# Two transformer blocks on one core: first attention scores inside the value projection, preparation spread over the head loop, low halves of some weights and sums of squares by other engines

## Chip, cores and metric

The kernel runs on one core of a Trainium2 chip. The metric is the device time of one execution in microseconds (us). Before the change it is 2415.28 us, the median of three runs (2414.47 to 2416.01). The profiled execution has a span of 2413.3 us from its first to its last instruction and a time of its own of 2415.17 us; the 1.9 us between them lie around the program. Five engines work side by side, each through its own instructions in order: TensorE (PE: matrix products and transposes), VectorE (DVE), ScalarE (ACT), GpSimd (POOL) and SyncE (SP, which issues loads). DMA engines move data; a DMA issued from POOL's queue can add into its destination.

## What is computed

Two residual networks, one behind the other, over 512 positions of width 1024, in float32. The first ("block 1", two layers) has differential attention and a gated linear recurrence, an MLP of width 4096 and a gate with a per-layer embedding; it ends with an RMS norm. The second ("block 2", two layers) is cut here to the part that the change touches:

```
hn   = rms_norm(h, g_pre_mix)
u, q, k, v, iq, ik, iw = split(hn @ w_in_2[l])          # the last three: the "index"
logits = einsum('qhd,sd->qhs', iq, ik) * IDX_DIM**-0.5
score  = einsum('qh,qhs->qs', iw, relu(logits))          # -inf for later chunks
top_idx = top_k(score, 128)                              # which keys a query may see
s = einsum('qhd,qkhd->qhk', q, k[top_idx]) * HEAD_DIM**-0.5
o = einsum('qhk,qkhd->qhd', softmax(s), v[top_idx])      # 8 heads of 64
y = pool_mixer(u)                                        # windowed means, a small product
h = h + norm(concat(y, o) @ w_out_2[l])
h = h + norm(square(relu(norm(h) @ w_ff1_2[l])) @ w_ff2_2[l])
```

The kernel does not gather: it computes all scores of a query and adds a bias that is a large negative number for each key outside the 128 highest index scores.

## The kernel before

**Split operands.** Each float32 factor is kept as a high half, which TensorE takes exactly, and a low half that holds the rest. A product of 128 by 128 weights with 512 columns is three matmuls: high by high, high by low, low by high. I call these three one *step*.

**Weights.** `PLAN` lists all pieces of weights in the order of use. `w_load` loads a piece into `raw` by SP's queue. `w_conv` makes `wh` (ACT, line 206) and `wl` in one of three ways: VectorE subtracts `raw - wh`; or ACT writes `-wh` (line 212) and a DMA from POOL's queue adds the piece from memory (line 215); or POOL subtracts in two halves (line 219). The second way is that of `w_in`, `w_out`, `w_in_2`, `w_out_2` and whatever is in `BY_DMA`; the third is that of the index pieces of layer 1.

**Order.** The order of TensorE's instructions is the order in which the Python code emits them (`Lane` chains them). `run(generator, n, at=...)` emits steps of a product and calls a hook behind the n-th; `weave(acts, g, n)` spreads a list of small acts over `n` steps of a generator. The other engines are ordered by the framework's scheduler by priority: what is emitted first goes first, unless `urgent` (or `tc.high_priority`) lifts it.

**Attention of block 2** is `mix2`. Behind the index scores VectorE chooses the 128 keys in 16 rounds for three groups of queries: `V.max` finds eight values, `V.match_replace` marks them; then three `tensor_scalar` turn the marks into the bias (tiles `ac`). Meanwhile TensorE runs the projections of k, q (`four(1024, ...)`) and v (`four(1536, ev_v)`). `prep_d`, `prep_q(j)` and `prep_k(j, c)` transpose two heads' queries and keys into `qs` and `ks` (ACT writes the high half, VectorE the low one). Before the change these stand as hooks in the v projection:

```
run(four(1536, ev_v), at={7: lambda: bcast(s_[:, 0:4], sb), 8: lambda: prep_d(0, 0),
                          9: lambda: prep_d(0, 1), 13: lambda: prep_q(0),
                          19: lambda: prep_k(0, 0), 25: lambda: prep_k(0, 1)})
```

Then a loop over 32 pairs of head and query tile follows: `sco` (scores on TensorE), `sof` (softmax: VectorE adds the bias and takes the maximum, ACT takes the exponential and normalizes, tile `xe`), `ptr` (TensorE transposes the weights; ACT and VectorE write the halves of `pt`), `pv` (the product with v). `weave` puts 66 steps of `fill()` between them, which are the projection of `u`, the pool mixer and half of `w_out_2`.

**Norms.** `Stat.add` squares a tile on ACT (tile `q`) and adds it to `acc` (VectorE, or POOL at line 423 with `eng=G`); `Stat.mean` sums `acc` over the partitions with a product against `ones`. `st4` and `st5` are the sums behind block 1's last gate and behind each block-2 layer. At the end of layer 0 of block 2, `index(0)` and `index(1)` run the next layer's index product for each half of the positions while the norm behind the MLP (`post_norm` on VectorE, with `split` into the tiles `X`) is still being finished; I call that stretch the index stage.

## Time and profile before

| | us |
|---|---|
| median of three runs | 2415.28 |
| the profiled execution | 2415.17 |
| its span | 2413.3 |
| TensorE busy | 2368.2 |
| VectorE busy | 1298.3 |
| ScalarE busy | 1189.6 |
| GpSimd busy | 266.9 |

TensorE is busy for 98% of the span, so its waits add up to some 45 us. A row of waits names the engine's line, the instruction that released it, the sum of the waits, how many there are and the longest. A row of a timeline gives the start, the time from the start of the first to the end of the last of the instructions that are shown together, engine, line, operation, output and inputs (without numbers), the shape and how many; in brackets the idle time before it and who ended it. Starts of matmuls that follow each other give the pace of the engine; their own durations overlap.

### The profile page before, as it was taken

The page shows a single profiled execution, that of the slowest core. Times are in us where ns is not written, and L with a number is a line of the kernel's source. Part 1 is how long each engine was busy: PE and PEld are TensorE (multiplying, and loading weights), DVE is VectorE, ACT ScalarE, POOL GpSimd, SP SyncE. Part 2 cuts the span into 40 slices and gives each one's busy share as a digit, 9 for nine tenths or more (in the row PEclk, how much of TensorE's full clock was granted, in tenths as well). Part 3 has the DMA queues.
Part 4 walks back from the last instruction along what each step waited for, and adds up shares of the span by engine and source line. Part 5 has one row for each costly group of instructions (what it writes and reads, how often), then busy time and mean ns, then how long its engine had stood idle before and what let it go on. Part 6 is the DMA issues. An engine that isn't in the chain of part 4 may idle for free.

```text
span 2413.3 us, 30955 instructions
## 1 busy us (share of the span) xinstructions
PE 2368.2 (98%) x11740; PEld 1987.3 (82%) x11740; DVE 1298.3 (54%) x2543; ACT 1189.6 (49%) x2028; POOL 266.9 (11%) x478
## 2 busy tenths in 40 slices
PE   9999999999999999999999999999999999999999
PEld 6878888888887888888888788888898878888888
DVE  8586433435458643344469857323337975532434
ACT  7785322424688532233366786323326588432422
POOL 3310000000131000000033120000014411000000
PEclk9999999999999999999999999999999999999999
DMA  7743333232874433233257554333325737333231
GB/s 201 177 100 107 103 97 96 92 100 88 192 175 98 113 96 96 91 101 96 83 136 161 118 132 121 97 96 96 96 79 141 164 82 171 92 97 97 95 104 54
DMA packets 79141, 273.31 MB, mean 113 GB/s; under 512 B 8848, under 2 KB 11280, under 8 KB 78992
## 3 DMA queue, kind: packets, MB, share of 16 engines
q1 hardware_dynamic: 62288, 211.22, 27.8%
q0 software_dynamic: 16704, 60.11, 14.3%
q8 instruction: 92, 1.51, 0.3%
q14 instruction: 57, 0.47, 0.1%
HBM read 269.20 MB, written 2.10 MB: 112 GB/s over the span
## 4 chain that ended last, share of the span: by engine, by line
PE 78%; DVE 11%; ACT 6%; issue 2%; POOL 1%; DMA 1%; SPq 0%; DVEq 0%; ACTq 0%; POOLq 0%
PE B L131 78%; DVE ac L131 2%; DVE m L131 2%; ACT xe L672 1%; DVE fo L131 1%; DVE xe L131 1%; DVE X L131 1%; ACT wh L206 1%; DVE rn L131 1%; ACT xe L1280 1%; ACT wl L212 1%; DVE h L131 1%; DVE pt L131 1%; ACT pt L1300 0%; DVE acc L131 0%
## 5 line engine op out<-in xcount | busy, mean ns | idle before, releaser
L131 PE MATMUL B<-X,wh 128*128 128x512 f32 (+1 forms) x3200 | 970.6, 386 | 0.1
L206 ACT ACTIVATE wh<-raw 128x1024 fp32r<-128x1024 f32 (+2 forms) x374 | 391.0, 1047 | 802.6 <-PE B L131 786.7
L131 DVE TENSOR_TENSOR wl<-raw,wh 128x1024 fp32r<-128x1024 f32 (+2 forms) x260 | 315.8, 1215 | 720.6 <-ACT wh L206 715.8
L131 PEld LDWEIGHTS B<-X,wh 128*128 128x128 f32 x3200 | 578.6, 189 | 104.0 <-issue 4.1
L131 PE MATMUL B<-X,wl 128*128 128x512 f32 (+1 forms) x1600 | 611.5, 382 | 2.8 <-POOL wl L219 1.8
L131 PE MATMUL B<-F,wh 128*128 128x512 f32 (+1 forms) x2048 | 597.8, 376 | 0.0
L131 PEld LDWEIGHTS B<-F,wh 128*128 128x128 f32 x2048 | 376.5, 188 | 70.0
L131 PE MATMUL B<-F,wl 128*128 128x512 f32 (+1 forms) x1024 | 384.8, 376 | 0.0
L131 PEld LDWEIGHTS B<-X,wl 128*128 128x128 f32 x1600 | 301.1, 188 | 62.5 <-POOL wl L219 2.6
L131 PE MATMUL B<-wh,X 128*128 128x512 f32 (+2 forms) x960 | 291.2, 380 | 0.0
L131 PEld LDWEIGHTS B<-F,wl 128*128 128x128 f32 x1024 | 192.8, 188 | 34.8
L131 PEld LDWEIGHTS B<-wh,X 128*128 128x128 f32 x960 | 176.4, 191 | 30.8 <-issue 1.9
L131 PE MATMUL B<-wl,X 128*128 128x512 f32 (+2 forms) x504 | 180.5, 371 | 3.1 <-DVE X L131 1.6
L215 POOL DMA_DIRECT2D wl<-in_w x105 | 92.0, 876 | 449.3 <-ACT wl L212 316.8
L212 ACT ACTIVATE wl<-raw 128x1024 fp32r<-128x1024 f32 (+2 forms) x108 | 112.6, 1043 | 41.3 <-PE B L131 41.2
L131 DVE TENSOR_TENSOR f<-r 128x512 f32<-128x512 f32 (+1 forms) x136 | 88.2, 656 | 59.6 <-ACT r L591 59.6
L591 ACT ACTIVATE r<-B 128x512 f32<-128x512 f32 (+1 forms) x136 | 76.3, 566 | 80.9 <-PE B L131 78.4
L131 PEld LDWEIGHTS B<-wl,X 128*128 128x128 f32 x504 | 93.5, 191 | 19.8 <-DVE X L131 2.2
L131 PE MATMUL B<-ks,qs 128*128 128x256 f32 (+2 forms) x352 | 84.3, 334 | 4.7 <-DVE qs L131 2.0
L131 DVE TENSOR_TENSOR F<-f,F 128x512 fp32r<-128x512 f32 (+1 forms) x136 | 88.3, 654 | 0.9 <-ACT F L397 0.2
L408 POOL TENSOR_TENSOR v<-v,nhalf 128x4 f32<-128x4 f32 x3 | 3.1, 1035 | 760.3 <-DVE v L131 760.3
L397 ACT ACTIVATE F<-f 128x512 fp32r<-128x512 f32 (+1 forms) x136 | 81.3, 604 | 4.2 <-DVE f L131 1.8
(224 smaller groups left out, 2412.4 us busy)
## 6 DMA issues: line engine op xcount, KB each, us to landing
raw<-in_w SPq DMA_DIRECT2D x379, 512.0 KB, 3.5
wl<-in_w POOLq DMA_DIRECT2D x105, 512.0 KB, 7.8
F<-in_w POOLq DMA_DIRECT2D x8, 512.0 KB, 10.7
raw<-in_wx SPq DMA_DIRECT2D x8, 328.0 KB, 2.9
h<-in_xT SPq DMA_DIRECT2D x8, 256.0 KB, 6.1
raw<-in_wx SPq DMA_DIRECT2D x8, 256.0 KB, 2.7
pt<-in_gates SPq DMA_DIRECT2D x2, 512.0 KB, 5.3
p<-in_pT SPq DMA_DIRECT2D x4, 256.0 KB, 2.9
```

The costliest lines, as they stand in the source:

```text
L131: r = f(*a, **k)
L206: g = A.activation(h_[:, :n], r[:, :n], AF.Copy)
L212: g = A.activation(l_[:, :n], r[:, :n], AF.Copy, scale=-1.0)
L215: G.dma_start(l_[:, :n], where[i], accum_op=OP.add)
L397: A.activation(dst[:, 0, :], src, AF.Copy)
L408: st["rsqrt"] = G.tensor_tensor(y, v, nhalf[:, :y.shape[-1]], op=OP.pow)
L591: A.activation(r_[:, :n], p_, AF.Relu)
L672: A.activation(e[:, :n], e[:, :n], AF.Exp, scale=-1.0, bias=mn, accum_out=sums)
L1280: A.activation(e[:, :n], e[:, :n], AF.Copy, scale=sm[:, 1:2])
```

## The change

It has six parts.

1. Low halves of all index pieces of layer 1 are made by ACT's negative copy and an adding DMA of POOL's queue in place of POOL's subtraction.
2. The pieces of `w_out_2` with `k >= 4` (four in each layer, 2 of them for each half of the columns) get their low half from VectorE in place of ACT and the adding DMA.
3. In block 1's last layer the sums `st4` and `st5` of the last four tiles are emitted behind the gate's product instead of within its evictions, and `st5` adds on VectorE in place of POOL; the pool of tiles has room for more of them.
4. In layer 0 of block 2 the sums `st4` are taken out of `nxt4` (where POOL added) and put into the last eight steps of `index(1)`, on VectorE.
5. The v projection is emitted behind the definitions, with new hooks: `prep_q(0)` at step 11 and `prep_k(0, 0)` at 15 (13 and 19 before), the scores and softmaxes of pairs 0 and 1 at 21, 22, 28 and 29. The loop starts at pair 0 with no empty acts ahead.
6. In the loop the preparation of the next two heads is spread from four neighbouring places over five of eight places, the last of them in the first place of those heads themselves.

```diff
-BY_DMA += [e for e in PLAN if e[0] == "index" and e[1] == 0][:3]
+BY_DMA += [e for e in PLAN if e[0] == "index" and e[1] == 0][:3] + [e for e in PLAN if e[0] == "index" and e[1] == 1]
...
         if (PLAN[i][0] in ON_POOL and PLAN[i][0] != "index" and i > 5
+                and not (PLAN[i][0] == "w_out_2" and PLAN[i][3] >= 4)
                 and PLAN[i][:4] != ("w_in_2", 0, 512, 0)) or PLAN[i] in BY_DMA:
...
-        elif PLAN[i][0] == "index" and PLAN[i][1] == 1 or i <= 5:
+        elif i <= 5:
             for a in range(0, n, n // 2):
                 b = slice(a, a + n // 2)
-                g = G.tensor_sub(l_[:, b], r[:, b], h_[:, b].bitcast(F32))
-                if "rsqrt" in st:
-                    behind(g, st["rsqrt"].ins)
+                G.tensor_sub(l_[:, b], r[:, b], h_[:, b].bitcast(F32))
...
-                L = Tags(lp, prj=(C512, F32, 8), t=(C512, F32, 3),
-                         q=(C512, F32, 2), sb=(C512, F32, 1))
+                L = Tags(lp, prj=(C512, F32, 8), t=(C512, F32, 6),
+                         q=(C512, F32, 4), sb=(C512, F32, 1))
...
+                    def sums(k):
+                        st4.add(h[k])
+                        if last:
+                            st5.add(h[k], scale=col("g_final", 0, k))
...
-                        st4.add(h[k])
-                        if last:
-                            st5.add(h[k], scale=col("g_final", 0, k), eng=G)
+                        if not last or g == 0:
+                            sums(k)
...
+                    if last and g == 1:
+                        for k in range(4, 8):
+                            sums(k)
...
-            run(four(1536, ev_v), at={7: lambda: bcast(s_[:, 0:4], sb), 8: lambda: prep_d(0, 0),
-                                      9: lambda: prep_d(0, 1), 13: lambda: prep_q(0),
-                                      19: lambda: prep_k(0, 0), 25: lambda: prep_k(0, 1)})
...
+            run(four(1536, ev_v), at={7: lambda: bcast(s_[:, 0:4], sb), 8: lambda: prep_d(0, 0),
+                                      9: lambda: prep_d(0, 1), 11: lambda: prep_q(0),
+                                      15: lambda: prep_k(0, 0), 21: lambda: sco(0), 22: lambda: urgent(sof)(0),
+                                      25: lambda: prep_k(0, 1), 28: lambda: sco(1), 29: lambda: urgent(sof)(1)})
             n = H2 * T
-            acts = [lambda: None] * 3
+            acts = []
...
-            for j in range(-2, n + 1):
+            for j in range(0, n + 1):
                 m, r = divmod(j, 8)
                 nx = 0 <= j < n - 8
-                if 0 <= j + 1 < n:
+                if 1 < j + 1 < n:
                     act(urgent(sof), j + 1)
...
-                if nx and r in (1, 2):
-                    act(prep_d, m + 1, r - 1)
-                if nx and r == 2:
+
+                if nx and r in (2, 6):
+                    act(prep_d, m + 1, r // 4)
+                if nx and r == 4:
                     act(urgent(prep_q), m + 1)
-                if nx and r == 3:
+                if nx and r == 5:
                     act(urgent(prep_k), m + 1, 0)
-                if nx and r == 4:
-                    act(urgent(prep_k), m + 1, 1)
+                if 8 <= j < n and r == 0:
+                    act(urgent(prep_k), m, 1)
...
                 split(X4[k][:, :, ts], h[k][:, ts], col("g_pre_mix_2", l + 1, k))
-                st4.add(h[k][:, ts], ts, eng=G)
...
-                run(index(1), at={7: f(1, 3, 4), 15: f(1, 5, 6), 23: f(1, 7)})
+                def sums(ts, *ks):
+                    for k in ks:
+                        st4.add(h[k][:, ts], ts)
...
+                run(index(1), at={7: f(1, 3, 4), 15: f(1, 5, 6), 23: f(1, 7),
+                                  **{24 + i: lambda i=i: sums(HALVES[i // 4], i % 4 * 2, i % 4 * 2 + 1)
+                                     for i in range(8)}})
```

How it moves instructions is shown at three places. The first is TensorE at the first scores of block 2's attention in layer 0 (`<-ks,qs`). `B` are its output banks, `wh`, `wl` the halves of a weight, `X` the activations. Before, the scores stand behind the last step of the v projection (`<-wh,X`), among steps of the projection of `u` (`<-X,wh`):

```order
L131 MATMUL B_10807<-wl_10809,X_9783 128x512
L131 MATMUL B_10807<-wh_10808,X_9783 128x512
L131 MATMUL B_10987<-X_9520,wh_10845 128x512 x2
L131 MATMUL B_10987<-X_9520,wl_10846 128x512
L131 MATMUL B_10999<-ks_10921,qs_10885 128x256 x2
L131 MATMUL B_10988<-X_9520,wh_10845 128x512 x2
```

After:

```order
L131 MATMUL B_10805<-wh_10749,X_9749 128x512
L131 MATMUL B_10805<-wl_10750,X_9749 128x512
L131 MATMUL B_10805<-wh_10749,X_9749 128x512
L131 MATMUL B_10930<-ks_10902,qs_10879 128x256 x2
L131 MATMUL B_10806<-wh_10749,X_9749 128x512
L131 MATMUL B_10806<-wl_10750,X_9749 128x512
L131 MATMUL B_10806<-wh_10749,X_9749 128x512
```

The scores have moved up past ten steps of the v projection, one step of `u` and one group of transposes. From the transposes of `sn` at the head of the last third of that projection to the first scores there were 25 steps and four groups of four transposes, that of `sn` counted; now there are 14 steps and three groups. Layer 1 has the same order.

The second place is VectorE at the end of the choice of keys in layer 0. The last row of the choice is `MATCH_REPLACE`, the three `TENSOR_SCALAR` make the bias, `qs` and `ks` are the low halves of the first two heads. Before:

```order
L131 MATCH_REPLACE ac_9807<-m_10644,ac_9807 128x512
L131 TENSOR_SCALAR ac_9805<-ac_9805 128x256
L131 TENSOR_SCALAR ac_9806<-ac_9806 128x384
L131 TENSOR_SCALAR ac_9807<-ac_9807 128x512
L131 TENSOR_TENSOR qs_10885<-B_10880,qs_10885 64x512
L131 TENSOR_TENSOR qs_10886<-B_10880,qs_10886 64x512
L131 TENSOR_TENSOR ks_10921<-B_10916,ks_10921 128x512
L131 TENSOR_TENSOR ks_10954<-B_10949,ks_10954 128x512
```

After:

```order
L131 MATCH_REPLACE ac_9807<-m_10644,ac_9807 128x512
L131 TENSOR_SCALAR ac_9805<-ac_9805 128x256
L131 TENSOR_SCALAR ac_9806<-ac_9806 128x384
L131 TENSOR_SCALAR ac_9807<-ac_9807 128x512
L131 TENSOR_TENSOR qs_10879<-B_10874,qs_10879 64x512
L131 TENSOR_TENSOR qs_10880<-B_10874,qs_10880 64x512
L131 TENSOR_TENSOR ks_10902<-B_10897,ks_10902 128x512
L131 ISA xe_10937,mn_10938<-B_10930,kbias 128x128
```

Up to the first `ks` VectorE's order is the same; behind it the first softmax (`ISA xe`) now comes ahead of the second `ks`.

The third place is POOL in the index stage. Before, it subtracts for the index pieces (line 219) and adds sums (line 423):

```order
L219 TENSOR_TENSOR wl_15168<-raw_14934,wl_15168 128x256 x2
L219 TENSOR_TENSOR F_14930<-raw_14915,F_14929 128x328 x2
L219 TENSOR_TENSOR F_15187<-raw_15172,F_15186 128x328 x2
L423 TENSOR_TENSOR acc_12460<-acc_12460,q_15115 128x256
L423 TENSOR_TENSOR acc_12460<-acc_12460,q_15122 128x256
L219 TENSOR_TENSOR wh_15221<-raw_15191,wh_15221 128x256 x2
L423 TENSOR_TENSOR acc_12460<-acc_12460,q_15154 128x256
```

After:

```order
L407 TENSOR_TENSOR rs_15037<-v_15035,nhalf 128x2
L216 DMA F_14926<-in_wx 128x656
L216 DMA wl_15154<-in_wx 128x512
L216 DMA F_15173<-in_wx 128x656
L216 DMA wh_15201<-in_wx 128x512
L216 DMA F_15220<-in_wx 128x656
```

POOL's tensor work has gone from this stretch; it issues DMAs there.

## Rows read from the trace of the kernel before

**Rows 1.** The page: busy time, share of the span and instructions of each engine.

```profile
PE 2368.2 (98%) x11740; PEld 1987.3 (82%) x11740; DVE 1298.3 (54%) x2543; ACT 1189.6 (49%) x2028; POOL 266.9 (11%) x478
```

**Rows 2.** Waits of TensorE, 1200 to 1440 us: waited for, sum, times, longest.

```profile
PE B L131 <- ACT xe L1280: 2.2, 2, 1.1
PE B L131 <- DVE pt L131: 2.1, 3, 1.1
PE B L131 <- DMA wl<-in_w: 1.0, 1, 1.0
PE B L131 <- DVE acc L131: 1.0, 1, 1.0
```

**Rows 3.** Waits of TensorE, 1790 to 2030 us.

```profile
PE B L131 <- ACT xe L1280: 3.3, 2, 2.2
...
PE B L131 <- DVE X L131: 1.6, 2, 1.3
PE B L131 <- ACT X L400: 1.5, 2, 0.9
...
PE B L131 <- DVE ks L131: 0.3, 1, 0.3
```

**Rows 4.** Timeline of TensorE, layer 0: four steps, transposes of sn, first scores.

```profile
1315.64 0.62 PE L131 MATMUL B<-wh,X 128*128 128x512 f32 x2
...
1318.36 0.39 PE L131 MATMUL B<-wh,X 128*128 128x512 f32 x1
1318.59 0.60 PE L131 MATMUL B<-ident,sn 128*128 128x128 f32 x4
...
1337.52 0.40 PE L131 MATMUL B<-ks,qs 128*128 128x256 f32 x2
```

**Rows 5.** Timeline of TensorE, layer 1: transposes of sn, first scores.

```profile
1906.86 0.60 PE L131 MATMUL B<-ident,sn 128*128 128x128 f32 x4
...
1926.73 0.39 PE L131 MATMUL B<-ks,qs 128*128 128x256 f32 x1 [0.27 <-DVE ks L131]
```

**Rows 6.** Engines by stretch, the choice of keys in both layers.

```profile
core 0: us, PE busy (x) PEld busy (x) DVE busy (x) ACT busy (x) POOL busy (x), PEclk, DMA share, GB/s
1286.00:1334.00 48.00, 48.00 (x221) 39.71 (x220) 48.00 (x147) 25.88 (x32) 21.38 (x49) 1.00 0.81 176
1875.60:1923.60 48.00, 48.00 (x221) 39.69 (x220) 48.00 (x147) 24.93 (x32) 20.52 (x48) 1.00 0.83 179
```

**Rows 7.** Timeline of VectorE behind the choice of keys, layer 0.

```profile
1334.07 0.90 DVE L131 TENSOR_SCALAR ac<-ac 128x256 f32<-128x256 f32 x3
...
1336.42 1.29 DVE L131 TENSOR_TENSOR ks<-B,ks 128x512 fp32r<-128x512 f32 x2
```

**Rows 8.** Engines by stretch: the granted clock behind waits.

```profile
1247.00:1250.40 3.40, 3.40 (x19) 3.40 (x18) 1.30 (x2) 0.20 (x1) 1.34 (x2) 0.52 0.57 204
...
1337.00:1350.00 13.00, 11.90 (x66) 9.58 (x65) 7.69 (x27) 11.38 (x27) 3.94 (x11) 1.00 0.53 124
...
1813.60:1817.00 3.40, 3.40 (x16) 3.40 (x15) 3.40 (x6) 1.46 (x4) 3.40 (x5) 0.52 0.39 127
...
1933.00:1936.40 3.40, 3.40 (x11) 2.67 (x10) 1.29 (x4) 2.10 (x5) 0.00 (x0) 0.53 0.00 0
```

**Rows 9.** Timeline of POOL at the end of block 1.

```profile
1244.16 1.30 POOL L423 TENSOR_TENSOR acc<-acc,q 128x512 f32<-128x512 f32 x1 [4.00 <-ACT q L422]
```

**Rows 10.** Timeline of VectorE in the index stage.

```profile
1804.75 0.47 DVE L131 SCALAR_TENSOR_TENSOR fo<-fo,par,sb 128x256 f32<-128x256 f32 x1
...
1806.69 1.99 DVE L131 SCALAR_TENSOR_TENSOR fo<-fo,par,sb 128x256 f32<-128x256 f32 x2
```

**Rows 11.** Timeline of POOL in the index stage.

```profile
1807.33 4.16 POOL L219 TENSOR_TENSOR F<-raw,F 128x328 fp32r<-128x328 f32 x4
```

**Rows 12.** Adding DMAs of index pieces, layer 0: KB, us to landing.

```profile
wl<-in_wx POOLq DMA_DIRECT2D x2, 256.0 KB, 5.8
```

## The prediction

> **What bounds the kernel now.** I read the busy times first: TensorE works for 2368.2 us of the span of 2413.3 [rows 1], so the engine whose waits count is TensorE, and what the change can win or lose is what it does to some 45 us of waits, and to TensorE's clock. The change leaves TensorE's instructions as they are in number and only moves some of them. Next come TensorE's waits in the two stretches that the change touches. From 1200 to 1440 us (end of block 1, attention of layer 0) the waits are 2.2 us for the softmax of ACT, 2.1 for `pt` of VectorE, 1.0 for a late low half that comes by DMA, 1.0 for `acc` [rows 2]. From 1790 to 2030 (index stage, attention of layer 1) they are 3.3 for the softmax, 1.6 and 1.5 for `X`, 0.3 for `ks` [rows 3], and for `pt` the same row as in the first stretch. Third comes the granted clock: three stretches of 3.4 us stand at 0.52 or 0.53 in place of 1.00, that is at 1.2 in place of 2.4 GHz [rows 8]. They begin 3 to 4 us behind waits: that for `acc`, those for `X`, and the wait of 2.2 us in layer 1's attention. Each costs 3.4 x 0.48 = 1.6 us. The same place in layer 0 has a wait of 1.1 us and a clock of 1.00.
>
> All sums are made against the profiled execution (2415.17 us, its span 2413.3 and 1.9 around it), which is within 0.2 us of the median of 2415.28.
>
> **First scores inside the v projection: the largest term.** In layer 0 four steps take 1318.36 - 1315.64 = 2.72 us, so 0.68 each. From the transposes of `sn` (1318.59) to the first scores (1337.52) there are 25 steps and four groups of transposes in 18.93 us [rows 4]; 25 x 0.68 = 17.0 leaves 0.48 for a group. After the change 14 steps and three groups lie between: 9.52 + 1.44 = 10.96 us. TensorE would reach the first scores at 1329.55 in layer 0, and in layer 1, from 1906.86 [rows 5], at 1917.82.
>
> What the scores need is another matter. They read the low half of `ks`, and VectorE writes it behind the whole choice of keys, the three bias instructions and the two `qs`; that order is the same as before. VectorE has no gap in the choice: 48.00 busy us of 48.00, in both layers [rows 6]. It ends at 1334.07; the pair of `ks` starts at 1336.42 and takes 1.29, so the first is there at 1337.07 [rows 7]. In layer 1 the first scores already waited for it and went on at 1926.73 [rows 5]. The start of the choice hangs on index scores that keep their place. So TensorE, whose queue is in order, stands still at the first scores with ten steps of the v projection queued behind them: 1337.07 - 1329.55 = 7.5 us in layer 0, 1926.73 - 1917.82 = 8.9 in layer 1. The steps that used to cover the choice now run behind it. Together **+16.4 us**. I see no cover for this: nothing that TensorE could do stands ahead of the scores.
>
> Behind them more work now lies between the first scores and their transposes (ten steps, 6.8 us), so the first softmax has time. Its waits before, the 1.1 and 2.2 that are the longest in their groups [rows 2, 3], and the 0.3 for `ks` go: -3.6. But ACT now has evictions of v between its softmaxes, and I take a wait of 1.0 behind the v projection in each layer, by the smaller of the two rows: +2.0. Net **-1.6** (bounds -3.6 to 0).
>
> The clock: layer 1 has its slow stretch already. In layer 0 a stop of 7.5 us is much longer than any that has brought one in the rows, so I add one: **+1.6** (bounds 0 and 3.2, one more in each layer). The Trainium skill, "TensorE: Matmul & The Clock Gate", section "What's actually happening", says that the throttled state is the default and that activity releases it; by it the slow stretch in layer 0 is due, as taken, while the 1.1 us wait with a clock of 1.00 shows that not every wait brings one; without that stretch the sum would be 1.6 lower.
>
> **Preparation in short blocks.** `prep_q` and `prep_k` bring transposes, an ACT copy and a VectorE subtraction each; spread over the loop they no longer come between neighbouring softmaxes. What they can give back is the wait for `pt`, 2.1 in each layer [rows 2]. The instructions stay, so I take half: **-2.1** (bounds 0 and -4.2). No DMA and no other queue takes part.
>
> **Late pieces of w_out_2 by VectorE.** The wait of 1.0 for the adding DMA in layer 0 [rows 2] goes; layer 1 has none: **-1.0**. VectorE must now subtract four pieces in each layer, and one of them stands ahead of the last `pt` half, which TensorE waits for; if it costs a wait like the longest one of that group, 1.1 in each layer, the term is +1.2. I keep -1.0, because ACT and POOL's queue lose the same pieces.
>
> **End of block 1.** TensorE waits 1.0 for `acc` [rows 2], and then the second sum hangs on POOL, whose last addition is 1244.16 + 1.30 = 1245.46 [rows 9]. With the sums on VectorE, where `acc` follows the last tile, I expect the wait gone and the slow stretch with it: -1.0 - 1.6 = **-2.6** (bounds 0 and -2.6; the additions on VectorE lie beside matmuls).
>
> **Index stage.** POOL's subtractions work there beside VectorE. One `fo` instruction takes 0.47 alone and two take 1.99, 1.0 each [rows 10], while POOL's block of four runs from 1807.33 for 4.16 us [rows 11]. VectorE feeds `X`, for which TensorE waits 1.6 + 1.5 [rows 3]. Without POOL's work I expect 2.2 of the 3.1 to go (the rest, the longest of the ACT waits, 0.9, stands behind ACT's copies, and those grow), and the slow stretch with it: -2.2 - 1.6 = **-3.8**. Against that, each low half now needs a copy by ACT and a DMA that lands 5.8 us after issue [rows 12], which VectorE's and POOL's path did not need; the pieces are used in this very stretch. At worst nothing is won and one wait of 1.0, like that for a DMA in [rows 2], comes on top: bounds -4.7 and +1.0. The sums moved into `index(1)` are sixteen short additions beside matmuls: 0.
>
> The Trainium skill, "SBUF — State Buffer", section "SBUF: two separate sides", warns against this part: a DMA issued from GpSimd's queue needs descriptors that GpSimd cannot write while VectorE holds their shared port in a two-port instruction. The row for layer 0 has 5.8 us to landing in a stretch where VectorE is busy, so by the rule that figure could grow; the sum would lose the index stage's 3.8 and come to about 2426.
>
> **The sum.** +16.4 - 1.6 + 1.6 - 2.1 - 1.0 - 2.6 - 3.8 = +6.9 us. 2415.2 + 6.9 = **2422 us**, 0.3% slower.
>
> **Rivals.**
>
> *No stop at the scores (faster).* If the choice of keys ended 7.5 to 9 us sooner, the scores would run where they are written, and the other terms stand alone: -1.6 - 2.1 - 1.0 - 2.6 - 3.8 = -11.1, so 2404. It decides at the moment when `ks` is ready: at or before 1329.6 in layer 0. For it speaks only that POOL works 21 of those 48 us beside VectorE [rows 6] and would have to be what stretches the choice; against it VectorE's unchanged order, and POOL's, which keeps that work. Chance 0.11.
>
> *The stop is paid back (within 0.2%).* While TensorE stands, ACT and VectorE lose nothing; they get further ahead, and the loop behind may run without its waits. The waits for softmax and `pt` are 2.2 + 2.1 and 3.3 + 2.1 in the two layers, 9.7 in all [rows 2, 3]. If they all vanish in place of my 3.7, the sum is 6.0 lower: 2416. Against it speaks that the loop's waits recur where a block of 512 keys is short of cover, late in the loop as well as early. Chance 0.29.
>
> *More is lost (slower).* The DMAs of the index pieces come late (no 3.8, and 1.0 more) and both layers get a further slow stretch in the attention (1.6 more): 2422 + 4.8 + 1.6 = 2428. It decides at the first matmul with a low half of the index pieces: whether it waits for a DMA. Chance 0.08.
>
> *The change does not do what it says.* The scores stand inside the projection, but they cannot run there; that is the forecast itself.
>
> **How the numbers follow.** The forecast has 0.52, at 2422. A measurement of this kernel can tell 0.2%, 4.8 us, from no change. Slower by more than that needs over 2420.1: the forecast and the last rival, 0.60. Within: 0.29. Faster: 0.11. The single bounds give 2415.5 (every gain at its best, no added slow stretch) to about 2430 (the gains of the index stage and of the end of block 1 lost); their far corner, all of it at once, lies higher but needs every term to miss. The range leaves out the faster rival and a little above: 2413 to 2430.
>
> **What would show it.** Right: in the changed kernel's trace a wait of 7 to 9 us at the first `B<-ks,qs` of each layer, released by VectorE's `ks`, at the end of the choice of keys; a slow stretch behind it in layer 0; no wait for `wl<-in_w` in the attention; no POOL additions at the end of block 1 and no slow stretch at 1247; shorter VectorE instructions and fewer waits for `X` in the index stage. Wrong: no such wait at the scores, or one that is released by another engine; or a choice of keys that ends well ahead of the scores; or waits for `wl<-in_wx` by DMA.

## Result and the profile after

The changed kernel takes 2437.32 us (median of four, 2436.28 to 2438.17) against 2415.27 of the kernel before in the same comparison: a ratio of 1.0091, 95% interval 1.0075 to 1.0107. It is 22 us slower. The forecast had the direction and its mechanism, but a third of the size, and the time lies 7 us above the range. The profiled execution has a span of 2436.4 us, 23.1 more than before.

The first line of the page after, beside [rows 1]: TensorE has 6.4 us more busy time (matmuls at half speed count as busy) and the rest of the 23 us is waiting. POOL has lost 37 us of work.

```profile
PE 2374.6 (97%) x11740; PEld 1991.8 (82%) x11740; DVE 1304.0 (54%) x2572; ACT 1186.8 (49%) x2028; POOL 229.8 (9%) x441
```

The waits of TensorE in the changed kernel from 1260 to 1440 us, that is layer 0's attention, with the columns of [rows 2] (waited for, sum, how many, longest):

```profile
PE B L131 <- DVE qs L131: 6.1, 1, 6.1
PE B L131 <- ACT ks L635: 3.1, 3, 1.5
PE B L131 <- ACT xe L1282: 1.9, 2, 1.4
PE B L131 <- DVE ks L131: 1.8, 4, 0.8
PE B L131 <- ACT pt L1302: 1.6, 1, 1.6
PE B L131 <- DVE pt L131: 0.6, 1, 0.6
```

Where [rows 2] had no `qs` or `ks` at all, they are now 11.0 of 15.1 us. The first row and one of 0.8 in the fourth are the stop at the first scores. The other waits for `ks` are 4.1 us at three places further down the loop (at each one for ACT's half and one for VectorE's), which the forecast did not have. In layer 1 the stop is 7.42 + 0.80, and the other waits repeat.

TensorE and VectorE at the stop in layer 0 of the changed kernel, two timelines (start, length, engine, operation, shapes, count, and in brackets the idle time before and its releaser):

```profile
1334.17 0.55 PE L131 MATMUL B<-ks,qs 128*128 128x256 f32 x1 [6.08 <-DVE qs L131]
1335.52 0.58 PE L131 MATMUL B<-ks,qs 128*128 128x256 f32 x1 [0.80 <-DVE ks L131]
```

```profile
1332.42 0.89 DVE L131 TENSOR_SCALAR ac<-ac 128x256 f32<-128x256 f32 x3
1333.34 1.41 DVE L131 TENSOR_TENSOR qs<-B,qs 64x512 fp32r<-64x512 f32 x2
1334.78 0.69 DVE L131 TENSOR_TENSOR ks<-B,ks 128x512 fp32r<-128x512 f32 x1
```

VectorE does what it did in [rows 7], at the same distance from the end of the choice of keys; TensorE now stands and watches it.

The granted clock, by stretches of the changed kernel (start and end, length, busy us of PE, PEld, DVE, ACT, POOL, then the clock, DMA share and GB/s), beside [rows 8]:

```profile
1200.00:1260.00 60.00, 59.94 (x353) 54.28 (x352) 43.65 (x87) 40.95 (x69) 10.69 (x13) 1.00 0.45 114
1330.60:1340.60 10.00, 5.63 (x14) 4.30 (x14) 5.24 (x16) 2.90 (x5) 0.97 (x3) 0.50 0.03 9
1439.80:1443.10 3.30, 3.01 (x14) 3.01 (x15) 0.72 (x2) 0.59 (x1) 0.00 (x0) 0.51 0.53 164
1931.30:1941.30 10.00, 6.11 (x15) 4.59 (x16) 4.75 (x14) 2.90 (x5) 1.46 (x5) 0.50 0.00 1
2040.50:2043.80 3.30, 3.23 (x15) 3.23 (x16) 0.70 (x2) 0.59 (x1) 0.00 (x0) 0.51 0.50 159
```

In this execution there is no slow stretch at the end of block 1. Each attention has two: one of 10.2 us, which begins while TensorE still stands at the first scores, and one of 3.4 us at the last waits of the loop.

That this is the change's doing is not shown. All five traces with the old sums (the kernel before and those with part 5, 6, 2 or the moved `prep_k` alone) have it, behind the wait of 1.0 for `acc`. But of the nine traces with part 3, in none of which that wait is left, four have it all the same (`e6_short_choice`, `e10_choice_14`, `e11_no_wout`, `e12_no_spread`). In the first of them, with the columns as above:

```profile
1200.00:1246.00 46.00, 45.94 (x263) 40.98 (x262) 33.63 (x55) 30.12 (x49) 4.17 (x6) 1.00 0.41 102
1246.10:1249.20 3.10, 3.10 (x16) 3.10 (x16) 1.07 (x2) 0.00 (x0) 1.76 (x1) 0.50 0.47 131
```

TensorE is busy for 45.94 of the 46 us ahead of it.

**The account.** Starts of the same matmuls in both traces give the shift from stretch to stretch: +1.1 up to 1183 us, -2.7 at the end of block 1, +14.5 in layer 0's attention, -3.9 in the index stage, +14.0 in layer 1's attention, 23.0 in all. The +1.1 stands in code that the change leaves alone; 0.9 of it comes with a slow stretch of 3.4 us at 764, which is in three traces here (the changed kernel's, `e5_urgent` and `e9_choice_15`) and not in the others. So the gains outside the attention came to the size that was forecast, 1.7 of them (the slow stretch at the end of block 1) by the luck of this execution, and all of the miss lies in the two attentions.

### The profile page after: what moved, and what is told of

The parts are those of the page before. It is cut to its first block, busy times and chain, and to the rows that moved or that the text cites. A ratio compares the mean times of both kernels' runs of the same rounds, so it can differ in the third digit from the quotient of the medians.

```text
span 2436.4 us, 30964 instructions
## 1 busy us (share of the span) xinstructions
PE 2374.6 (97%) x11740; PEld 1991.8 (82%) x11740; DVE 1304.0 (54%) x2572; ACT 1186.8 (49%) x2028; POOL 229.8 (9%) x441
## 4 chain that ended last, share of the span: by engine, by line
PE 80%; DVE 11%; ACT 5%; issue 2%; DMA 1%; POOL 1%; SPq 0%; DVEq 0%; ACTq 0%; POOLq 0%
PE B L131 80%; DVE ac L131 2%; DVE m L131 2%; ACT xe L671 1%; DVE xe L131 1%; DVE rn L131 1%; ACT wh L206 1%; DVE ks L131 1%; DVE X L131 1%; DVE pt L131 1%; DVE fo L131 1%; ACT wl L213 1%; DVE acc L131 0%; DVE qs L131 0%; DVE h L131 0%
## 5 line engine op out<-in xcount | busy, mean ns | idle before, releaser
L131 DVE TENSOR_TENSOR wl<-raw,wh 128x1024 fp32r<-128x1024 f32 (+2 forms) x268 | 324.6, 1212 | 721.5 <-ACT wh L206 717.4
L213 ACT ACTIVATE wl<-raw 128x1024 fp32r<-128x1024 f32 (+2 forms) x103 | 105.9, 1029 | 41.2 <-PE B L131 41.2
L216 POOL DMA_DIRECT2D wl<-in_w x97 | 85.0, 877 | 428.9 <-ACT wl L213 304.7
L131 PEld LDWEIGHTS B<-ks,qs 128*128 128x128 f32 x352 | 61.9, 190 | 46.9 <-issue 15.7
## 6 DMA issues: line engine op xcount, KB each, us to landing
F<-in_w POOLq DMA_DIRECT2D x8, 512.0 KB, 10.2
```

What stands on the lines that cost most here:

```text
L131: r = f(*a, **k)
L213: g = A.activation(l_[:, :n], r[:, :n], AF.Copy, scale=-1.0)
L216: G.dma_start(l_[:, :n], where[i], accum_op=OP.add)
```

## Experiments

Each kernel was timed beside the kernel before, in whose own runs the median moved between 2415.5 and 2416.1. Times below are medians; ratios are against the kernel before, with their 95% interval.

**Parts alone: the sums and the index pieces.** The kernel before with parts 1, 3 and 4:

```diff
-BY_DMA += [e for e in PLAN if e[0] == "index" and e[1] == 0][:3]
+BY_DMA += [e for e in PLAN if e[0] == "index" and e[1] == 0][:3] + [e for e in PLAN if e[0] == "index" and e[1] == 1]
...
+                        if not last or g == 0:
+                            sums(k)
...
-                st4.add(h[k][:, ts], ts, eng=G)
```

> The kernel before with parts 1, 3 and 4 alone (index pieces by ACT and DMA, sums behind the gate and behind the norm). Theory: the gains of the end of block 1 (2.7) and of the index stage (3.8) are real and stand by themselves: 2415.3 - 6.5 = 2408.8. Rival: they are gains only on paper, the index stage gives them back as later waits in the attention of layer 1: 2413 or above.

2409.95 us, ratio 0.9975 (0.9964 to 0.9986). The gains stand by themselves: 6.2 us. Starts of matmuls moved by -1.0 at the end of block 1 by the sums and by 1.7 more behind it (the slow stretch, which this execution has not either), and by -4.4 at the first half of the index stage; 1.1 came back in its second half and 1.1 in the attention of layer 1, there mostly as a wait of 0.8 for the DMA of `w_out_2`.

**Parts alone: the first scores.** The kernel before with part 5:

```diff
+                                      9: lambda: prep_d(0, 1), 11: lambda: prep_q(0),
+                                      15: lambda: prep_k(0, 0), 21: lambda: sco(0), 22: lambda: urgent(sof)(0),
+                                      25: lambda: prep_k(0, 1), 28: lambda: sco(1), 29: lambda: urgent(sof)(1)})
...
-            for j in range(-2, n + 1):
+            for j in range(0, n + 1):
```

> The kernel before with part 5 alone (first scores inside the v projection, loop starting at pair 0). Theory: the stop at the first scores costs 7 us in layer 0 and 8 in layer 1, and a slow stretch of some 10 us behind it costs 3 in each; the waits of 1.1 and 2.5 at the first softmax go and layer 1's old slow stretch with them: about +15 to +16, 2431, with the loop's waits behind as before. Rival: the new waits inside the loop come from this part, by the loop's shifted phase: about +22 to +28, 2440, with waits of 1.2 to 1.5 at scores of the later heads.

2428.67 us, ratio 1.0052 (1.0037 to 1.0067), 12.5 us slower. The stops are 6.09 + 0.80 and 7.41 + 0.80, the slow stretches behind them 10.2 and 6.8 us. No wait for `ks` follows in the loop, but the end of the loop is longer, with waits of 1.35 and 1.56 (more on it below). So this part makes the stop and the slow stretch, as the theory had it (with 2.5 to 3.5 us less), and the loop's waits for `ks` are not its doing.

**Parts alone: the spread preparation.** The kernel before with part 6:

```diff
-                if nx and r == 3:
+                if nx and r == 5:
                     act(urgent(prep_k), m + 1, 0)
-                if nx and r == 4:
-                    act(urgent(prep_k), m + 1, 1)
+                if 8 <= j < n and r == 0:
+                    act(urgent(prep_k), m, 1)
```

> The kernel before with part 6 alone (preparation of the next two heads spread, the last prep_k in the first place of those heads). Theory: each pair of heads now waits for ks at its first scores, 4.1 us in each layer, and the waits for pt (2.0 in each layer) go: about +4, 2419, with waits for ks at scores three times in each layer. Rival (the step of the forecast): the waits for pt go and nothing comes in their place: about -2 to -4, 2412.

2432.24 us, ratio 1.0067 (1.0052 to 1.0082): 16 us slower, where the forecast had a gain and even the theory only 4 us of loss. TensorE's waits behind the first scores in layer 0, from 1345 to 1440:

```profile
PE B L131 <- ACT ks L636: 2.1, 3, 1.1
PE B L131 <- DVE pt L131: 1.9, 4, 1.0
PE B L131 <- ACT xe L672: 1.7, 1, 1.7
PE B L131 <- DVE ks L131: 1.7, 3, 0.7
PE B L131 <- ACT pt L1300: 1.6, 1, 1.6
PE B L131 <- ACT xe L1280: 1.3, 1, 1.3
```

In the kernel before these rows are 2.1 for `pt` of VectorE [rows 2], 0.7 for `pt` of ACT and 1.1 of the softmax waits. The wait for `pt` is almost what it was; the 3.8 for `ks` came on top, a wait of 1.7 at a product of the pool mixer (the row that names an exponential of ACT), a longer end of the loop, and one more slow stretch in each layer.

**Parts alone: the late pieces of w_out_2.** The kernel before with part 2:

```diff
+                and not (PLAN[i][0] == "w_out_2" and PLAN[i][3] >= 4)
```

> The kernel before with part 2 alone (late pieces of w_out_2 by VectorE). Theory: the wait of 1.0 for the DMA in layer 0 goes, but VectorE's subtraction ahead of the last pt half makes the waits at the end of the attention 1.8 longer in each layer, and a slow stretch of 3.4 us follows in each (1.7): about +3 to +6, 2419. Rival (the step of the forecast): -1.0, 2414.3.

2421.77 us, ratio 1.0022 (1.0013 to 1.0032), 5.6 us slower. The wait for the DMA goes, as forecast; it is gone with part 5 alone and with part 6 alone as well, so that part 2 is what removes it in the changed kernel is not shown. But the end of the loop is longer (below), and a wait of 1.4 for `qs` comes in each layer. What VectorE and ACT do at the end of the loop in the changed kernel:

```profile
1436.03 1.21 ACT L1253 ACTIVATE X<-B 128x256 f32<-128x256 f32 x4
1437.09 1.09 ACT L206 ACTIVATE wh<-raw 128x1024 fp32r<-128x1024 f32 x1
1438.03 0.63 ACT L1302 ACTIVATE pt<-B 128x512 fp32r<-128x512 f32 x1
```

```profile
1438.21 1.22 DVE L131 TENSOR_TENSOR wl<-raw,wh 128x1024 fp32r<-128x1024 f32 x1 [1.48 <-ACT wh L206]
1439.35 0.68 DVE L131 TENSOR_TENSOR pt<-B,pt 128x512 fp32r<-128x512 f32 x1
```

In the kernel before, ACT wrote the last `pt` from 1425.99 and this `wh` behind it, from 1426.48:

```profile
1425.99 0.60 ACT L1300 ACTIVATE pt<-B 128x512 fp32r<-128x512 f32 x1
1426.48 1.05 ACT L206 ACTIVATE wh<-raw 128x1024 fp32r<-128x1024 f32 x1
```

In the changed kernel the conversion of 1.09 stands ahead of `pt` on ACT, and the subtraction of 1.22 ahead of its low half on VectorE. TensorE's last three waits of the loop grow from 1.08 + 0.69 + 0.34 to 1.36 + 1.56 + 0.99, in the kernel with part 2 alone as in the changed kernel. The last two of them, before and after:

```profile
1426.64 0.38 PE L131 MATMUL B<-pt,vv 128*128 128x256 f32 x1 [0.69 <-ACT pt L1300]
1427.36 1.10 PE L131 MATMUL B<-pt,vv 128*128 128x256 f32 x7 [0.34 <-DVE pt L131]
...
1438.72 0.38 PE L131 MATMUL B<-pt,vv 128*128 128x256 f32 x1 [1.56 <-ACT pt L1302]
1440.09 1.86 PE L131 MATMUL B<-pt,vv 128*128 128x256 f32 x7 [0.99 <-DVE pt L131]
```

The swap on ACT, with waits of 1.35 + 1.56, is in the traces of parts 5, 6 and 2 alone, all three; only the 0.99 belongs to part 2.

**The order of VectorE at the stop.** Parts 1, 3, 4 and 5, and the first preparation marked urgent:

```diff
-                                      9: lambda: prep_d(0, 1), 11: lambda: prep_q(0),
-                                      15: lambda: prep_k(0, 0), 21: lambda: sco(0), 22: lambda: urgent(sof)(0),
+                                      9: lambda: prep_d(0, 1), 11: lambda: urgent(prep_q)(0),
+                                      15: lambda: urgent(prep_k)(0, 0), 21: lambda: sco(0), 22: lambda: urgent(sof)(0),
```

> Parts 1, 3, 4 and 5, with the first prep_q and prep_k marked urgent, so that VectorE writes the low halves of the first qs and ks between two rounds of the choice of keys and not behind it. Theory: the stop at the first scores is VectorE's order and nothing else; it goes (15 us), and with it the slow stretches behind it; the waits of 1.1 and 2.5 at the first softmax are gone too. From the 2410.0 of parts 1, 3 and 4: about 2406. Rival: the scores or the softmax cannot get on before the choice has ended, which now ends 3 us later: a wait of 6 us or more comes at the second softmax in place of the stop, 2418 or more.

2409.01 us, ratio 0.9974 (0.9962 to 0.9986). VectorE in this kernel, layer 0: the low halves now lie between rounds of the choice, and the bias (`TENSOR_SCALAR`) behind them.

```profile
1324.50 1.41 DVE L131 TENSOR_TENSOR qs<-B,qs 64x512 fp32r<-64x512 f32 x2
...
1328.24 0.69 DVE L131 TENSOR_TENSOR ks<-B,ks 128x512 fp32r<-128x512 f32 x1
...
1335.04 1.85 DVE L131 TENSOR_SCALAR ac<-ac 128x256 f32<-128x256 f32 x3
```

Of the stop a wait of 0.73 is left (0.47 in layer 1), and no slow stretch comes there. ACT writes the high half of the first `ks` from 1324.46, where the changed kernel has 1324.41. So the same instructions, in another order on one engine, take the stop away: the cause is VectorE's order. But against parts 1, 3 and 4 alone nothing is won beyond the uncertainty. From the transposes of `sn` to the end of the attention, layer 0 is as long as before (0.0) and layer 1 0.6 shorter: the waits of 1.1 and 2.25 at the first softmax have gone, a wait of 0.84 and one of 1.48 for a softmax came a little later, and the end of the loop has the swap on ACT.

**A shorter choice.** The changed kernel with 12 in place of 16 rounds (it leaves out 32 of the 128 keys):

```diff
-            for _ in range(TOPK // 8):
+            for _ in range(TOPK // 8 - 4):
```

> The changed kernel, with 12 in place of 16 rounds of the choice of keys (it leaves 32 of the 128 chosen keys out, so its output differs; 12 us of VectorE's work are gone in each layer). Theory: VectorE's choice is what TensorE stands still for; the stop of 6.9 and 8.2 goes, and the slow stretch of 10.2 us behind it (2.9 in each layer): 2437.3 - 15.1 - 5.8 = 2416.5. Rival: the half-speed stretch is not due to the stop, or the waits come back at the next place: 2422 or more; if the choice were not the gate at all: 2437.

2417.64 us, ratio 1.0009 (0.9999 to 1.0018): 19.7 less than the changed kernel, the theory had 20.9. The stop and the slow stretch behind it have gone in both layers, and the waits of the loop are all still there (for `ks` 3.1 of ACT and 1.0 of VectorE, the end of the loop 1.35 + 1.56 + 0.99). They are therefore neither due to the stop nor hidden by it.

**Spread, with distance.** The kernel before, with only the second `prep_k` (and its `prep_d`) moved:

```diff
-                if nx and r in (1, 2):
-                    act(prep_d, m + 1, r - 1)
+                if nx and r in (1, 4):
+                    act(prep_d, m + 1, r // 4)
...
-                if nx and r == 4:
+                if nx and r == 6:
                     act(urgent(prep_k), m + 1, 1)
```

> The kernel before with the preparation spread over the loop, but prep_q and the first prep_k left in their old places (2 and 3 of eight) and only the second prep_k moved, to place 6, four places ahead of its scores. Theory: the 3.7 us of waits for ks in each layer of e3_spread come from a first prep_k that stands one place, and a second that stands two places, ahead of the scores that need them; they go: 2432.2 - 7.4 = 2425 if the later waits and the added slow stretch stay, down to 2415 if those go as well. Rival: any spreading costs the waits, because ACT is late with ks wherever it stands: 2430 or more.

2420.63 us, ratio 1.0019 (1.0010 to 1.0029): 11.6 less than part 6 alone, more than the waits for `ks`, but still 4.8 us slower than the kernel before. Its waits from 1345 to 1440:

```profile
PE B L131 <- DVE xe L131: 2.2, 2, 1.5
PE B L131 <- DVE pt L131: 1.7, 4, 0.8
PE B L131 <- ACT xe L1280: 1.1, 1, 1.1
PE B L131 <- ACT pt L1300: 0.7, 1, 0.7
PE B L131 <- DVE ks L131: 0.2, 1, 0.2
```

The waits for `ks` have gone but for 0.2; the end of the loop has its old length, and there is no added slow stretch (even the old one of layer 1's attention is not there, though its wait of 2.2 is). A wait of 1.5 at the pool mixer's product remains. So it is the distance between preparation and use that made the waits for `ks`, not the spreading. Spreading itself takes 0.4 off `pt` and does not win: this milder form of it costs 4.8 us.

**Both repairs together**: `e5_urgent` with the places of `e7_spread_slack`.

```diff
+                if nx and r in (1, 4):
+                    act(prep_d, m + 1, r // 4)
...
+                if nx and r == 6:
                     act(urgent(prep_k), m + 1, 1)
```

> e5_urgent with the spread of e7_spread_slack added. Theory: it differs from e5_urgent by what e7_spread_slack differs from the kernel before. Rival: the two interact, because in e5_urgent the loop starts with ACT further ahead: it is faster than e5_urgent even if e7_spread_slack is slower than the kernel before.

2410.96 us, ratio 0.9981 (0.9971 to 0.9990). Its interval overlaps with that of `e5_urgent`; whether the spread adds or takes time here is not told. The theory, 4.8 us more than `e5_urgent`, did not come (2.0 more by the medians).

**How the slow stretch goes with the stop.** The changed kernel with 15 rounds (below) and with 14 (`- 2` in the same place):

```diff
-            for _ in range(TOPK // 8):
+            for _ in range(TOPK // 8 - 1):
```

> The changed kernel with 15 in place of 16 rounds of the choice (8 of the 128 chosen keys left out). The stops should be one round, 3.0 us, shorter: 3.9 and 5.2. Theory: the slow stretch grows with the stop, so more than 5.9 us come back: 2428 to 2431, with half speed for less than 10 us. Rival: the slow stretch has one length whatever the stop is: 2437.3 - 5.9 = 2431.4, or, if it stays until the stop's length is made up by work, none of it.

> The same with 14 rounds: stops of 1.0 and 2.3 us. Theory: 11.8 us of stops and nearly all of the 5.8 us of half speed come back, 2420 to 2422; layer 0, with a stop of 1.0, has no slow stretch there. Rival: any stop at this place brings the 10 us stretch: 2425.

2432.39 us (ratio 1.0069, 1.0052 to 1.0086) and 2424.73 (1.0039, 1.0024 to 1.0054). From 16 to 15 rounds 4.9 us come back, to 14 another 7.7, to 12 another 7.1. The stops of layer 0 and the slow stretch there are 6.9 and 10.2 us with 16 rounds, 3.9 and 6.8 with 15, 1.2 and none with 14. In layer 1 they are 8.2 and 10.2, 5.3 and 6.8, 2.5 and 3.4. So the slow stretch grows with the stop. That one round gave less than its 5.9 us and the next more has to do with further stretches: with 15 rounds one of 3.4 stands in each layer behind a wait or two of the loop (at 1412 and 1958), which the changed kernel does not have. Two stretches of the 15-round and the 14-round kernel, in this order, with the columns as above:

```profile
1330.00:1336.60 6.60, 4.60 (x11) 3.57 (x12) 2.87 (x7) 2.19 (x5) 0.00 (x0) 0.50 0.13 53
```

```profile
1326.00:1336.00 10.00, 8.83 (x42) 6.90 (x41) 5.32 (x15) 3.93 (x7) 2.10 (x6) 1.00 0.64 139
...
1355.50:1358.70 3.20, 3.20 (x12) 2.72 (x11) 0.84 (x4) 1.27 (x4) 0.31 (x1) 0.51 0.37 73
```

With 14 rounds the place of the stop runs at 1.00, and a slow stretch stands some 25 us further on, behind one of the loop's waits for `ks`.

**Parts taken out of the changed kernel.** Without part 2 (the first line), and in a second kernel without part 6 (the others):

```diff
-                and not (PLAN[i][0] == "w_out_2" and PLAN[i][3] >= 4)
...
-                if nx and r == 5:
+                if nx and r == 3:
                     act(urgent(prep_k), m + 1, 0)
-                if 8 <= j < n and r == 0:
-                    act(urgent(prep_k), m, 1)
+                if nx and r == 4:
+                    act(urgent(prep_k), m + 1, 1)
```

> The changed kernel without part 2 (the late w_out_2 pieces by ACT and DMA as before). Alone, part 2 cost 5.6 us. Theory: most of that is the order of ACT's tail, which parts 5 and 6 bring as well, so here only the wait of 1.0 behind VectorE's subtraction goes and a wait for the DMA comes back: 2435 to 2438. Rival: part 2 costs the same here as alone: 2431.7.

> The changed kernel without part 6 (the preparation of the next heads in the old four neighbouring places). Theory: the waits for ks in the loop, 4.1 us in each layer, go, and the stops and the tail stay: 2437.3 - 8.2 = 2429. Rival: part 6 costs here what it costs alone, 16 us: 2421.

2438.03 us without part 2 (ratio 1.0092, 1.0077 to 1.0107): the same as the changed kernel, so part 2 costs nothing there that the runs can tell. Of what it cost alone, the swap on ACT (some 1.1 us in each layer) is there without it, since parts 5 and 6 bring it too; the wait of 1.4 for `qs` in each layer is not in the changed kernel; the 0.99 of its own goes back to 0.34. 2428.75 us without part 6 (ratio 1.0055, 1.0040 to 1.0070): the theory had 2429. Part 6 costs 8.6 us within the change.

## Why the forecast was wrong

The direction and the largest term were right; the size was wrong by 15 us, and two terms had the wrong sign. Per term, forecast against the traces of before and after (both layers together where there are two):

| term | forecast | measured |
|---|---|---|
| stop at the first scores | +16.4 | 6.88 + 8.22 = +15.1 |
| waits at the first softmax | -1.6 | -3.6 |
| clock in the attentions | +1.6 | +7.7 |
| preparation in short blocks (all waits in the loop) | -2.1 | +6.4 |
| late pieces of w_out_2 (end of the loop) | -1.0 | +2.6 |
| end of block 1 | -2.6 | -2.7 |
| index stage | -3.8 | -3.9 |
| sum | +6.9 | +21.6 |

The measured column comes to 21.6; with the +1.1 ahead of the touched code it is 22.7 of the 23.1 by which the span grew.

*The stop.* Right in cause and within 1.3 us in size. It is shown from three sides: VectorE's order alone takes it away (`e5_urgent`), fewer rounds take it away (`e6_short_choice`), and each round is worth 3 us of it (`e9_choice_15`). The rival by which the choice would be over in time is out. So is the one by which other waits would pay the stop back: with part 5 alone the waits within layer 0's loop went from 2.0 to 1.2, where it needed some 3 us in each layer.

*The first softmax.* The step "a wait of 1.0 behind the v projection" did not come in the changed kernel. In `e5_urgent`, where TensorE does not stand, it does come, with 0.84 and 1.48: while TensorE stood, ACT had time. The forecast counted a price that only the faster version pays.

*The clock.* This is the first step that failed. I took one slow stretch of 3.4 us in layer 0, since all three rows in [rows 8] had that length; but those stood behind waits of some 1 to 2 us, and the stop was to be three times longer. They begin "3 to 4 us behind waits" only if one counts from the start of a wait (from its end it is 0.6 to 2.7 us), so that a stop of 7 us could hold the beginning of its own. The bounds did not hold it either. In the traces the stretch is 10.2 us long in both layers and begins inside the stop; of it, 4.3 and 3.8 us are spent standing, and the moving 5.9 and 6.4 cost half of themselves, 2.9 and 3.2. The Trainium skill, "TensorE: Matmul & The Clock Gate", section "What's actually happening", has the throttled state as the default that activity releases; the trace agrees in that the clock falls during the stop, and the runs with 15 and 14 rounds give the lengths; the stretch at 1246 of `e6_short_choice`, behind 45.94 busy us of 46, does not fit it. Two further stretches of 3.4 at the longer end of the loop add 1.6 each, and layer 1's old one (1.6) is gone: 2.9 + 3.2 + 3.2 - 1.6 = 7.7.

*Preparation in short blocks.* The second step that failed, and the largest: -2.1 became +6.4. I counted the instructions and their engines and found them unchanged, and asked only whose way they would be out of; I did not ask how far each one stands from its reader. In the loop, scores run two places ahead of the transposes (`sco` of pair j + 2 in place j). The first `prep_k` at place 5 therefore stands one place ahead of the first scores of its heads, at 6, and the second, at place 0, two places ahead of the scores at place 2. TensorE's rows in the changed kernel at one such spot: the transposes (six, of which four are the preparation's), one step, and then the wait for what ACT and VectorE make of them.

```profile
1410.42 0.82 PE L131 MATMUL B<-ident,xe 128*128 128x128 f32 x6
1410.99 0.71 PE L131 MATMUL B<-X,wh 128*128 128x512 f32 x2
1411.54 0.40 PE L131 MATMUL B<-X,wl 128*128 128x512 f32 x1
1413.42 0.39 PE L131 MATMUL B<-ks,qs 128*128 128x256 f32 x1 [1.49 <-ACT ks L635]
1414.15 0.39 PE L131 MATMUL B<-ks,qs 128*128 128x256 f32 x1 [0.34 <-DVE ks L131]
```

This was to be read from the diff and from VectorE's and ACT's durations: a copy of 0.6 and a subtraction of 0.69 behind the transposes do not fit beside a step of 0.68. ACT's own queue adds to it: from the end of the transposes (1411.24) the copy waits behind parts of two softmaxes, with `pt` between them.

```profile
1411.29 0.62 ACT L1282 ACTIVATE xe<-xe,sm 128x384 f32<-128x384 f32 x1
1411.80 0.38 ACT L1302 ACTIVATE pt<-B 128x256 fp32r<-128x256 f32 x1
1412.06 0.73 ACT L671 ACTIVATE xe<-xe,mn 128x512 f32<-128x512 f32 x1
...
1412.77 0.60 ACT L635 ACTIVATE ks<-B 128x512 fp32r<-128x512 f32 x1
```

In the second half of [rows 7] the pair of `ks` has its price, and it was used only for the first scores. `e7_spread_slack` shows that distance is the cause, and `e12_no_spread` that the waits for `ks` go with part 6.

*Late pieces of w_out_2.* The third step that failed. I had the harmful order in hand (the subtraction ahead of the last `pt` half) and a bound of +1.2 in sum, and kept -1.0 "because ACT and POOL's queue lose the same pieces". ACT's own order, with a conversion of 1.05 moved ahead of the last `pt`, was not in the sum at all. The wait of 1.0 for the DMA went, and the end of the loop grew by 1.8 in each layer. Of these 1.8 only the 0.65 at the low half hang on part 2; the other 1.1 are ACT's swap, which `e11_no_wout` has too. So the row of the table is a place in the loop, and no term of the forecast held what parts 5 and 6 do there.

*End of block 1 and index stage.* At the end of block 1 the wait of 1.0 for `acc` went, as forecast, in every trace with part 3. The 1.6 for the slow stretch came by luck: the forecast took that stretch to hang on the wait, and four of the nine traces have it without the wait. The index stage is right in size, and its slow stretch is in none of the nine traces with the new index pieces. The cause fits, though no run takes POOL's work away alone. In the index stage VectorE's pair of `fo` instructions takes 0.88 where it took 1.99 in [rows 10]:

```profile
1819.04 0.88 DVE L131 SCALAR_TENSOR_TENSOR fo<-fo,par,sb 128x256 f32<-128x256 f32 x2
```

No wait for `X` is left there. What came instead is small, from 1780 to 1840 us of the changed kernel:

```profile
PE B L131 <- DMA F<-in_wx: 1.5, 2, 1.1
```

The Trainium skill, "SBUF — State Buffer", section "SBUF: two separate sides", had warned of adding DMAs behind VectorE's two-port work. They did land later than in layer 0's row, after 7.4 to 8.4 us in place of 5.8 [rows 12]; whether the port is the reason no run here shows, and TensorE paid 1.5 us for it, not the whole gain.

**What stays open.** Why the framework's scheduler puts the `wh` conversion ahead of the last `pt` in three different edits was not tried; only that it does, and what it costs. The costs alone (12.5, 16.1, 5.6, less 6.2) add up to 28 and not to 22: `e11_no_wout` and `e12_no_spread` show the overlap for parts 2 and 6, but not wait by wait.

**A better version.** Parts 1, 3 and 4 alone beat both kernels (0.9975), and so does `e5_urgent` (0.9974). These two are not told apart, so the smaller edit is the one to take.

## To carry to other kernels

Moving work of the bounding engine ahead of a gate is worth nothing unless the gate moves too: look up what the moved instruction reads, which engine writes that, and what stands ahead of the writer in its own queue. For a preparation that is moved within a loop, count the places to its first reader, not the instructions, and look at what stands in the writer's queue between them. Price a long stop with the half speed behind it, and do not take its length from rows behind short waits.

## What had not been expected of the hardware

The half-speed stretch was not of one length. Behind the first scores it was 10.2 us or 6.8 us with stops of 6.9 and 8.2 us (the kernels with part 5 alone, without part 2 and without part 6 have one of each, the last the other way round), 6.8 with stops of 3.9 and 5.3, 3.4 with 2.5, and none with 1.2. In the changed kernel it began about 2.5 us into the stop of layer 0 and went on for 5 us behind it. And a wait does not tell whether a stretch follows: 1.0 for `acc` at the end of block 1 has one behind it [rows 2, 8], the 1.1 at the first softmax of layer 0 has none; the 2.2 at the first softmax of layer 1 has one in four traces and none in `e7_spread_slack`; and the stretch at 1246 comes in four traces with no wait ahead of it.
